# Experts' first products with the weights stationary in float16, and scatters cut to the rows set aside

## The chip, the cores and the metric

The kernel runs on one core of a Trainium2 chip. The metric is the device time of one execution in microseconds, as the median of the timed runs.

## The reference

One layer of a hybrid encoder over 2048 tokens of width 1024, with float32 inputs. The first sub-layer mixes tokens (latent attention, gated delta rule, pooling), projects, and ends in a layer norm. The second, on which this case turns, is a mixture of 32 experts in 4 groups:

```
h = x * (1.0 + sc2) + sh2
g_p, g_sel = lax.top_k(softmax(hf @ w_rg + b_rg), 1)          # one group of 4
e_p, e_idx = lax.top_k(softmax(logits of that group), 2)      # two experts of its 8
weights = g_p * e_p / jnp.sum(e_p, axis=-1, keepdims=True)
y[t] = sum over its two experts e of
       weights * ((silu(h[t] @ w_gate[e]) * (h[t] @ w_up[e])) @ w_down[e])
x = layer_norm(DEEPNORM_ALPHA * x + (1.0 + gt2) * y, ln2_g, ln2_b)
```

w_gate and w_up are 1024 x 256 per expert, w_down is 256 x 1024. There are 4096 assignments of a token to an expert.

## The kernel before

The program is one stream of instructions, written as Python generators; a planner orders each engine's instructions by expected durations and priority, and an engine then runs its queue in order. Only instructions marked `keep_in_program_order` stay where they are written.

The stages are: the input projection, the attention beside the delta rule, the output projection with the first norm and the routing (`phase_c`, some 1100 to 1345 us), the experts (`experts`, to 1848 us), and the final norm (`combine`). All matmuls on float32 data are done as three products of a high and a low part (`split`: ACT rounds the high part, DVE or POOL subtracts the low one), so that the sum is nearly exact.

Per tile of 128 tokens, `norm` (L1305) makes the experts' input h from the norm's rows g2 and b2, writes it to `s_h` in memory (L1325), and writes the residual, scaled, to `s_x1` (L1329). `route_tokens` and `routing` choose the experts, sort the experts by load into 32 places, and give each place a fixed number of blocks of 128 rows: three for places 0 and 1, two up to place 12, one beyond, 47 blocks in all. Rows without a token carry indices past the end: the gather skips them, and the scatter writes them to spare rows.

For each expert, `expert_load` (L1627) brings three pieces of 1 MB over SP's queue into one of two sets of three slots, and `expert_split` (L1636) cuts them into high and low parts (ACT and DVE, six pieces of 128 x 1024 each). A block is then:
- `gather` (L1647): POOL issues an indirect transfer of the block's rows of `s_h` into one of three buffers.
- `block_in` (L1662): eight float32 transposes on TensorE, and two splits of 128 x 512 out of PSUM into b_xH and b_xL.
- `block_gate` (L1673): 24 matmuls; the tokens are stationary and 512 columns of gate and up weights move. ACT takes the silu, DVE multiplies into b_hs.
- `block_mid` (L1686): two transposes of b_hs, and a split.
- `block_out` (L1696): 12 matmuls of 512 columns with w_down moving, scaled into b_yo by ACT and POOL (first half) and DVE (second half); then POOL issues an indirect transfer that adds b_yo's rows into `s_x1` (L1712).

TensorE's order in the steady loop (L1780) is: gate and up products of block n, transposes of block n + 1, down products of block n - 1. The work tiles (b_yo, b_hs and others) lie in two pools that alternate by block, with one buffer of b_yo in each. All scatters add into the same `s_x1`, so each one waits for the one before it. `overflow_tables` (L1808) prepares a loop (`overflow`, L1855) for experts that exceed their blocks; the loop's number of turns is read from data at the end.

## Time and profile before

| what | us |
|---|---|
| median of 3 runs (1896.87 to 1903.39) | 1901.23 |
| span of the profiled execution, first to last instruction | 1905.1 |
| TensorE busy in it | 1695.9 |
| VectorE busy in it | 1450.5 |
| ScalarE busy in it | 1019.4 |
| GpSimd busy in it | 792.0 |

The page of the profile gives a time for the profiled execution by its span alone. In the page PE is TensorE's matmuls and PEld its weight loads, DVE is VectorE, ACT ScalarE, POOL GpSimd, SP the engine that issues most transfers; L1712 is a line of the kernel. A row of a group has the number of instructions behind an x, then their busy time and the mean of one, then the idle time ahead of them. Matmuls overlap, so the mean of one is longer than the distance between two.

### The profile page before, as it was taken

The numbers are of one execution on the slowest core, as the hardware profiler recorded it, in microseconds if no ns is written. First come the engines' busy times: TensorE is split into PE (matmuls) and PEld (weight loads), VectorE is DVE, ScalarE is ACT, GpSimd is POOL, SyncE is SP. The second block draws the span as 40 slices with busy tenths as digits, with TensorE's granted clock in tenths as the row PEclk, the third lists the DMA queues.
The fourth block names the chain that finished last, engine by engine and source line by source line (L and its number), as shares of the span: only waits on it lengthen the run. The fifth ranks groups of instructions, "written<-read, shape, count | busy, mean of one in ns | idle before, by whom it ended". The sixth has DMA issues, their size and how long they took to land. (4 is left out here: it accounts for less than half of the span.)

```text
span 1905.1 us, 30525 instructions
## 1 busy us (share of the span) xinstructions
PE 1695.9 (89%) x10849; PEld 1341.0 (70%) x10849; DVE 1450.5 (76%) x2579; ACT 1019.4 (54%) x1785; POOL 792.0 (42%) x662
## 2 busy tenths in 40 slices
PE   6998999988999899999999798997689999999950
PEld 5776777666767687878777587776567788777740
DVE  7767667587878978777776387778579998988958
ACT  5522431256877787466667533233256666665737
POOL 0101126421667834344344353434424455544437
PEclk9999999999998999999999899998799999999985
DMA  9564123654432232332202643451398999999958
GB/s 350 177 200 152 67 75 119 195 171 166 119 83 65 54 71 65 95 81 79 69 26 75 206 166 134 144 189 68 126 323 249 313 306 307 310 292 306 324 123 339
DMA packets 173163, 322.71 MB, mean 169 GB/s; under 512 B 77617, under 2 KB 102737, under 8 KB 160716
## 3 DMA queue, kind: packets, MB, share of 16 engines
q1 hardware_dynamic: 151872, 261.33, 40.3%
q0 software_dynamic: 19008, 59.28, 12.3%
q8 instruction: 86, 1.41, 0.3%
q14 instruction: 69, 0.56, 0.1%
q10 hardware_dynamic: 2128, 0.13, 0.1%
HBM read 239.20 MB, written 89.01 MB: 172 GB/s over the span
## 5 line engine op out<-in xcount | busy, mean ns | idle before, releaser
L818 POOL TENSOR_TENSOR t_pL<-t_pt,t_pH 128x512 f16<-128x512 f32 (+3 forms) x153 | 158.1, 1037 | 232.6 <-ACT t_pH L816 144.7
L699 DVE TENSOR_REDUCE t_mp<-t_px 128x1 f32<-128x512 f32 (+2 forms) x320 | 190.6, 606 | 59.6 <-PE t_px L697 58.4
L815 ACT ACTIVATE t_pt<-t_stt 128x512 f32<-128x512 f32 (+1 forms) x320 | 172.1, 538 | 115.4 <-PE t_stt L811 101.4
L186 PE MATMUL a_mm<-hH,a_wH 128*128 128x512 f32 x448 | 182.6, 411 | 15.4 <-ACT hH L176 14.7
L120 DVE TENSOR_TENSOR e_w1L<-e_w,e_w1H 128x1024 fp32r<-128x1024 f32 x126 | 169.6, 1373 | 23.5 <-ACT e_w1H L119 23.4
L119 ACT ACTIVATE e_w1H<-e_w 128x1024 fp32r<-128x1024 f32 x128 | 133.1, 1063 | 85.0 <-PE b_pg L1680 65.3
L186 PE MATMUL a_mm<-hL,a_wH 128*128 128x512 f32 x448 | 171.8, 399 | 0.1
L816 ACT ACTIVATE t_pH<-t_stt 128x512 f16<-128x512 f32 (+1 forms) x320 | 171.5, 536 | 0.1
L186 PE MATMUL a_mm<-hH,a_wL 128*128 128x512 f32 x416 | 164.9, 399 | 2.2 <-DVE a_wL L120 2.2
L785 PEld LDWEIGHTS <-t_pH 128*128 128x128 f16 x2176 | 120.5, 99 | 59.6 <-issue 46.9
L1712 POOL DMA_INDIRECT s_x<-b_yo,q_idx x47 | 80.0, 1702 | 192.8 <-DMA s_x<-b_yo,q_idx 86.5
L1680 PE MATMUL b_pg<-e_w1H,b_xH 128*128 128x512 f32 x376 | 155.4, 413 | 0.5 <-ACT b_xH L119 0.5
L809 PE MATMUL t_stt<-qH,kH 96*128 96x512 f32 (+2 forms) x320 | 145.8, 456 | 7.2 <-ACT t_pH L816 7.2
L1680 PE MATMUL b_pg<-e_w1H,b_xL 128*128 128x512 f32 x376 | 151.5, 403 | 0.0
L1680 PE MATMUL b_pg<-e_w1L,b_xH 128*128 128x512 f32 x376 | 150.5, 400 | 0.0
L818 DVE TENSOR_TENSOR t_pL<-t_pt,t_pH 128x512 f16<-128x512 f32 (+3 forms) x167 | 121.0, 726 | 35.7 <-ACT t_pH L816 34.7
L785 PE MATMUL t_pv<-vH,t_pH 128*128 128x65 f16 x1088 | 138.1, 198 | 2.6 <-DVE t_yt L791 2.6
L785 PE MATMUL t_pv<-vH,t_pL 128*128 128x65 f16 x1088 | 134.8, 196 | 1.2 <-DVE t_pL L818 0.8
L697 PE MATMUL t_px<-kH,qH 96*128 96x512 f32 (+2 forms) x320 | 122.9, 393 | 13.0 <-DVE t_mp L699 11.0
L785 PE MATMUL t_pv<-vL,t_pH 128*128 128x65 f16 x1088 | 133.2, 194 | 0.0
L810 PE MATMUL t_stt<-qL,kH 96*128 96x512 f32 (+1 forms) x320 | 121.4, 379 | 0.0
L811 PE MATMUL t_stt<-qH,kL 97*128 97x512 f32 (+1 forms) x320 | 120.9, 378 | 0.0
(489 smaller groups left out, 4789.7 us busy)
## 6 DMA issues: line engine op xcount, KB each, us to landing
e_w<-moe_w SPq DMA_DIRECT2D x96, 1024.0 KB, 9.0
m_w<-w_modT SPq DMA_DIRECT2D x48, 512.0 KB, 4.4
c_xs<-x SPq DMA_DIRECT2D x16, 512.0 KB, 4.3
c_ys<-s_y SPq DMA_DIRECT2D x16, 512.0 KB, 5.0
s_h<-c_h SPq DMA_DIRECT2D x16, 512.0 KB, 2.6
s_x<-c_r SPq DMA_DIRECT2D x16, 512.0 KB, 2.6
f_x<-s_x SPq DMA_DIRECT2D x16, 512.0 KB, 10.1
out_dram<-f_x SPq DMA_DIRECT2D x16, 512.0 KB, 4.9
```

The source lines that it names most:

```text
L119: return (self.nc.scalar.activation(hi, src, AF.Copy), (eng or self.nc.vector).tensor_tensor(lo, src, f32(hi) if hi.dtype == F32R else hi, ...
L120: (eng or self.nc.vector).tensor_tensor(lo, src, f32(hi) if hi.dtype == F32R else hi, op=ALU.subtract))
L186: nc.tensor.matmul(pt, a[:, k, :], b[k][:, cc * CH:(cc + 1) * CH], start=k == 0 and n == 0, stop=k == KD - 1 and n == len(ops) - 1)
L697: pin(nc.tensor.matmul(px[:, 0:w], qH[0:r, t * P:(t + 1) * P], kH[e][0:r, kb * CH:kb * CH + w], start=True, stop=True))
L699: pin(v.reduce_max(mp[:, t, kb:kb + 1], px[:, 0:w], axis=AX.X))
L785: nc.tensor.matmul(pv[:, t, :], a[:, ts_], b[:, j, h, :], start=j == 0 and t == 0 and i == 0, stop=j == nj - 1 and t == 3 and i == 2, skip ...
L809: nc.tensor.matmul(st[:, off:], kH[e][0:r, js], qH[0:r, off:], start=True, stop=False)
L810: nc.tensor.matmul(st[:, off:], kH[e][0:96, js], qL[0:96, off:], start=False, stop=False)
L815: nc.scalar.activation(pt[:, off:], st[:, off:], AF.Exp, scale=SCALE)
L816: nc.scalar.activation(pH[:, off:], st[:, off:], AF.Exp, scale=SCALE)
L818: eng.tensor_tensor(pL[:, off:], pt[:, off:], pH[:, off:], op=ALU.subtract)
L1680: nc.tensor.matmul(pg, a[:, k], b[:, k], start=k == 0 and i == 0, stop=k == KD - 1 and i == 2)
```

## The change

Places get their own number of rows, in steps of 16 (`ROWS`, 4720 rows in all, still 47 blocks); an expert's one or two blocks become one unit of up to 256 rows, except that the three blocks of the first expert stay units of their own. For gate and up, the weights become stationary, in float16 high and low parts of the weights times 256, and the unit's tokens move, so the result comes out transposed already and `block_mid` goes. For that, `norm` scales h by a power of two and stores it as float16 high and low parts; `block_in` transposes those and copies them out of PSUM. Of the two pieces of w_down, the low part of one is now subtracted by POOL. The scatter moves only the rows set aside, and takes its indices through a column that tells whether the block's last element is finite; at the end, the loop for overflowing experts also redoes all blocks if a row was not. The work pools alternate by unit instead of by block. Weight pieces go through eight slots in turn instead of two sets of three; there are four gather buffers instead of three. The overflow tables have a tile of their own instead of borrowing b_yo.

The core of the diff:

```diff
-R3, R2 = 2, 13
-CAP = [3] * R3 + [2] * (R2 - R3) + [1] * (32 - R2)
+
+ROWS = [384] + [256] * 2 + [224, 208] + [192] * 2 + [176] * 5 + [160, 144] + [128] * 4 + [112] * 6 + [96] * 2 + \
+    [80] * 4 + [64] * 2
+CAP = [-(-n // 128) for n in ROWS]
+R3, R2 = CAP.index(2), CAP.index(1)
 NB = sum(CAP)
+
+NOV = 40
+
+WSC = 256.0
...
+            sig = self.sig = rp.tile([P, 4], F32, name="c_sig")
+            for i, src in enumerate((g2, b2)):
+                nc.scalar.activation(sc2, src, AF.Abs)
+                v.tensor_reduce(sig[:, i:i + 1], sc2, axis=AX.X, op=ALU.max)
+            v.tensor_scalar(sig[:, 0:1], sig[:, 0:1], sig[:, 1:2], 2.0 ** -60, op0=ALU.add, op1=ALU.max)
+            si = sig.bitcast(I32)
+            v.tensor_scalar(si[:, 0:1], si[:, 0:1], 0x7F800000, None, op0=ALU.bitwise_and)
+            v.tensor_scalar(si[:, 1:2], si[:, 0:1], float(13 << 23), None, op0=ALU.subtract)
+            v.tensor_scalar(si[:, 0:1], si[:, 0:1], -1.0, float(267 << 23), op0=ALU.mult, op1=ALU.add)
+            v.tensor_scalar(sig[:, 2:3], sig[:, 1:2], 1.0 / WSC, None, op0=ALU.mult)
+            nc.scalar.activation(g2, g2, AF.Copy, scale=sig[:, 0:1])
+            nc.scalar.activation(b2, b2, AF.Copy, scale=sig[:, 0:1])
+            self.identh = rp.tile([P, P], F16, name="c_identh")
+            v.tensor_copy(self.identh, c["ident"])
...
-                xs = X.pop(t)
-                r = wk.tile([P, D], F32, tag="r", name="c_r")
+                r = X.pop(t)
+                tmp = wk.tile([P, CH], F32, tag="r", name="c_r", bufs=1)
                 sums = wk.tile([P, 2], F32, tag="sum", name="c_sum")
                 for j in range(2):
                     js = slice(j * CH, (j + 1) * CH)
-                    v.tensor_tensor(r[:, js], pp.pop((t, j)), gt1[:, js], op=ALU.mult)
-                    v.scalar_tensor_tensor(r[:, js], xs[:, js], ALPHA, r[:, js], op0=ALU.mult, op1=ALU.add,
+                    v.tensor_tensor(tmp, pp.pop((t, j)), gt1[:, js], op=ALU.mult)
+                    v.scalar_tensor_tensor(r[:, js], r[:, js], ALPHA, tmp, op0=ALU.mult, op1=ALU.add,
                                            accum_out=sums[:, j:j + 1])
                 s = wk.tile([P, 5], F32, tag="ln", name="c_ln")
-                sq = wk.tile([P, D], BF, tag="lnq", name="c_lnq", bufs=1)
+                hx = wk.tile([P, 2, D], F16, tag="hx", name="c_hx", bufs=1)
...
-                nc.sync.dma_start(io["s_h"][sl, 0:D], h[t])
+                self.split(hx[:, 0], hx[:, 1], h[t], g_)
+                nc.sync.dma_start(io["s_h"][sl, 0:D], hx.rearrange("p a d -> p (a d)").bitcast(F32))
...
+        def first(k):
+            src, dst = w1[k // 4][:, k % 4:k % 4 + 2], slice(k, k + 2)
+            nc.scalar.activation(H[0][:, dst], src, AF.Copy, scale=WSC)
+            nc.vector.scalar_tensor_tensor(H[1][:, dst], src, WSC, H[0][:, dst], op0=ALU.mult, op1=ALU.subtract)
+        todo = [lambda k=k: first(k) for k in range(0, KD, 2)]
+        todo += [lambda k=k, e=e: self.split(H[2][:, k], H[3][:, k], w2[:, k], e)
+                 for k, e in enumerate((nc.gpsimd, nc.vector))]
...
+    def block_in(self, ps, x, off, xg):
+
         nc = self.nc
-        pg = ps.tile([P, CH], F32, tag="b_g", name="b_pg")
-        for k in range(KD):
-            if half and k == KD // 2:
+        m = xg.shape[0]
+        xh = xg[:, 0:D].bitcast(F16)
+        for i, copy in enumerate((lambda o, s: nc.scalar.activation(o, s, AF.Copy), nc.vector.tensor_copy)):
+            pt = ps.tile([P, KD, P], F16, tag="c_t", name="b_pt")
+            for k in range(KD):
+                nc.tensor.transpose(pt[:, k, 0:m], xh[:, i * D + k * P:i * D + (k + 1) * P], self.identh[0:m, 0:m])
+            copy(x[i][:, :, off:off + m], pt[:, :, 0:m])
+
+    def unit_gate(self, wk, ps, W, x, n, half=None):
...
+            pg = ps.tile([P, 2, 256], F32, tag="b_g", name="b_pg")
+            for j in range(2):
+                fs = slice((2 * j + f) * P, (2 * j + f + 1) * P)
+                for k in range(KD):
+                    for i, (a, b) in enumerate(((0, 0), (1, 0), (0, 1))):
+                        nc.tensor.matmul(pg[:, j, 0:n], W[a][:, k, fs], x[b][:, k, 0:n],
+                                         start=k == 0 and i == 0, stop=k == KD - 1 and i == 2)
+            hs = wk.tile([P, 256], F32, tag="hs", name="b_hs", bufs=2)
+            nc.scalar.activation(hs[:, 0:n], pg[:, 0, 0:n], AF.Silu, scale=inv)
+            nc.vector.scalar_tensor_tensor(hs[:, 0:n], pg[:, 1, 0:n], inv, hs[:, 0:n], op0=ALU.mult, op1=ALU.mult)
+            self.split(hH[:, f, 0:n], hL[:, f, 0:n], hs[:, 0:n])
...
+    def block_out(self, wk, ps, W, h, w, ms, col, first=False):
+
+        R, v = self.R, self.nc.vector
+        m = ms.stop - ms.start
+        yo = wk.tile([P, D], F32, tag="yo", name="b_yo")
+        self.block_rows(wk, ps, W, h, w, ms, yo, first)
+        ix = wk.tile([P, 1], I32, tag="ix", name="b_ix", bufs=2)
+        v.tensor_scalar(R["fin"][0:m, col:col + 1], yo[0:m, D - 1:D], 0.0, 0.0, op0=ALU.mult, op1=ALU.is_equal)
+        v.tensor_scalar(ix[0:m], R["dsp"][0:m, col:col + 1], R["fin"][0:m, col:col + 1], self.spare[0:m],
+                        op0=ALU.mult, op1=ALU.add)
+        self.scatter(yo[0:m], ix[0:m])
...
+        blocks, units = [], []
+        for i, r in enumerate(order):
+            bs = [(sum(CAP[:r]) + b, min(P, ROWS[r] - b * P)) for b in range(CAP[r])]
+            for u in ([b] for b in bs) if i == 0 else [bs]:
+                units.append((i, range(len(blocks), len(blocks) + len(u))))
+                blocks += u
+        slots = self.slots
+        loaded = [1]
...
+        def out(u, W, h, w, first=False):
+            off = 0
+            for n, wn in zip(units[u][1], w):
+                m = blocks[n][1]
+                self.block_out(wks[u % 2] if u > 1 else wks[0], ps, W, h, wn, slice(off, off + m), blocks[n][0], first)
+                off += m
...
+            h = self.unit_gate(wks[u % 2], ps, W[i], x, n)
+            if u == 4:
+                self.overflow_tables(rp, wks[u % 2])
             wn = w
-            if n + 1 < len(blocks):
-                x, w = block_in(n + 1)
-            if n + 3 < len(blocks):
-                self.gather(XG[n % 3], idx(n + 3))
-            for f in now[0::2]:
+            if u + 1 < len(units):
+                x, n, w = unit_in(u + 1)
+                gather(units[u + 1][1].stop + 4)
+            for f in todo[0::2]:
                 f()
             if prev:
-                self.block_out(wk(prev[0]), ps, *prev[1:])
-            h = self.block_mid(wk(n), pt, hs)
-            for f in now[1::2]:
+                out(*prev)
+            for f in todo[1::2]:
                 f()
-            prev = (n, W[i], h, wn, idx(n))
-        self.block_out(wk(prev[0]), ps, *prev[1:])
+            todo = []
+            prev = (u, W[i], h, wn)
+        out(*prev)
...
+        e32 = wk.tile([P, NOV, 32], F32, tag="ov", name="v_e32")
...
+            dsp = R["dsp"][:, 0:NB]
+            v.scalar_tensor_tensor(redo[:, 0:NB], R["fin"][:, 0:NB], 0.0, dsp, op0=ALU.is_equal, op1=ALU.mult)
+            v.memset(redo[:, NB:], 0.0)
+            v.tensor_scalar(redo, redo, self.spare, None, op0=ALU.add)
+            v.tensor_scalar(junk, redo, S + 0.5, 0.0, op0=ALU.is_lt, op1=ALU.add, accum_out=anyc[:, 0:1])
+            with ExitStack() as ep:
+                ps = ep.enter_context(self.pool(name="o_p0", bufs=1, space=PSUM))
+                pa = ps.tile([P, 1], F32, name="o_pa")
+                nc.tensor.matmul(pa, self.c["ones"], anyc[:, 0:1], start=True, stop=True)
+                v.tensor_scalar(anyc[:, 1:2], pa, 0.0, None, op0=ALU.is_gt)
+            flag = anyc[:, 1:2]
+            v.scalar_tensor_tensor(tab, R["tA"], flag, R["tB"], op0=ALU.mult, op1=ALU.add)
+            v.tensor_copy(tabi[:, 0:NB + NOV], tab[:, 1])
+            v.scalar_tensor_tensor(tabi[:, NB + NOV:], flag, float(NB), R["tot"], op0=ALU.mult, op1=ALU.add)
+            nov = nc.values_load(tabi[0:1, NB + NOV:NB + NOV + 1], min_val=0, max_val=NB + NOV)
```

## Rows read from the trace of the kernel before

**Rows 1.** Busy us by stage, PE to POOL; clock, DMA share, GB/s.

```profile
1100.00:1345.00 245.00, 219.29 (x1120) 181.62 (x1119) 193.48 (x412) 81.70 (x118) 111.03 (x87) 0.94 0.41 140
1415.00:1848.00 433.00, 408.98 (x1938) 329.23 (x1938) 384.02 (x494) 260.63 (x380) 202.95 (x126) 0.98 0.92 284
1500.00:1800.00 300.00, 290.76 (x1402) 234.49 (x1401) 273.40 (x337) 192.73 (x280) 147.61 (x92) 1.00 0.98 306
```

**Rows 2.** Chain that ended last, one block: start us, us, what.

```profile
1494.90 5.61 PE b_pg L1680 x24
1500.51 0.87 PE b_pt L1669 x8
1501.39 2.61 PE b_py L1704 x12
```

**Rows 3.** POOL's timeline: two neighbours, first and last of 38; [idle before].

```profile
1436.13 1.60 POOL L1712 DMA_INDIRECT s_x<-b_yo,q_idx  x1 [0.28 <-POOL b_yo L1709]
...
1497.38 1.59 POOL L1712 DMA_INDIRECT s_x<-b_yo,q_idx  x1 [6.37 <-DMA s_x<-b_yo,q_idx]
...
1504.27 1.59 POOL L1712 DMA_INDIRECT s_x<-b_yo,q_idx  x1 [1.96 <-DVE b_hs L1683]
...
1803.88 1.59 POOL L1712 DMA_INDIRECT s_x<-b_yo,q_idx  x1 [6.90 <-DVE b_wc L1658]
```

**Rows 4.** DMA view, 1497.4 and 1500:1800: count, us to landing.

```profile
s_x<-b_yo,q_idx POOLq DMA_INDIRECT x1, 6.1
...
s_x<-b_yo,q_idx POOLq DMA_INDIRECT x30, 9.0
```

**Rows 5.** Waits between 1415 and 1848: us in total, times, longest us.

```profile
ACT b_yo L1708 <- DMA s_x<-b_yo,q_idx: 39.1, 24, 2.7
...
DVE b_yo L1706 <- DMA s_x<-b_yo,q_idx: 15.5, 11, 1.9
```

**Rows 6.** Float16 in the attention: TensorE's timeline, and its loads as a group.

```profile
804.53 0.19 PE L785 MATMUL t_pv<-vH,t_pH 128*128 128x65 f16 x1
804.56 0.19 PE L785 MATMUL t_pv<-vH,t_pL 128*128 128x65 f16 x1
...
L785 PEld LDWEIGHTS <-t_pH 128*128 128x128 f16 x2176 | 120.5, 99 | 59.6 <-issue 46.9 <-DVE t_yt L791 5.0 <-DVE n_rt L1162 0.5
```

**Rows 7.** DMA view of the last scatter, 1847:1856.

```profile
q0 software_dynamic: 144, 0.52, 36.7%
...
s_x<-b_yo,q_idx POOLq DMA_INDIRECT x1, 6.2
```

**Rows 8.** First scatter's ACT and POOL timelines, 1358 to 1361 us.

```profile
1358.18 0.69 ACT L1708 ACTIVATE b_yo<-b_py,b_wc 128x512 f32<-128x512 f32 x1 [0.76 <-PE b_py L1704]
...
1360.51 1.69 POOL L1712 DMA_INDIRECT s_x<-b_yo,q_idx  x1 [0.30 <-POOL b_yo L1709]
```

**Rows 9.** Groups by line in 1100:1345, ACT and POOL.

```profile
L119 ACT ACTIVATE c_yH<-c_ys 128x1024 fp32r<-128x1024 f32 x14 | 14.8, 1055 | 69.7 <-PE c_pp L1280 54.5 <-DVE q_l L1579 12.3 <-DMA s_h<-c_h 2.8
...
L120 POOL TENSOR_TENSOR e_w1L<-e_w,e_w1H 128x1024 fp32r<-128x1024 f32 x2 | 4.9, 2448 | 0.0
```

**Rows 10.** DVE's timeline around the overflow tables.

```profile
1403.32 1.21 DVE L120 TENSOR_TENSOR e_w1L<-e_w,e_w1H 128x1024 fp32r<-128x1024 f32 x1
1412.04 0.69 DVE L1826 TENSOR_TENSOR v_e<-q_cnt,iotas 128x512 f32<-128x512 f32 x1 [7.52 <-DMA s_x<-b_yo,q_idx]
```

**Rows 11.** DVE's groups by line in 1500:1800.

```profile
L120 DVE TENSOR_TENSOR e_w2L<-e_w,e_w2H 128x1024 fp32r<-128x1024 f32 x42 | 54.6, 1300 | 2.0 <-ACT e_w2H L119 2.0
L120 DVE TENSOR_TENSOR b_xL<-b_pt,b_xH 128x512 fp32r<-128x512 f32 x60 | 38.2, 675 | 0.0
```

**Rows 12.** DVE's group in the final norm, 1855:1905.

```profile
L1929 DVE SCALAR_TENSOR_TENSOR f_x<-f_x,f_s,r_ln_g 128x1024 f32<-128x1024 f32 x16 | 19.9, 1277 | 17.1 <-DMA f_x<-s_x 17.0
```

**Rows 13.** POOL's and DVE's timelines at 1544.6.

```profile
1544.64 1.85 POOL L1709 TENSOR_TENSOR b_yo<-b_yo,r 128x512 f32<-128x512 f32 x1
...
1544.78 1.73 DVE L1658 SCALAR_TENSOR_TENSOR b_wc<-b_xg,q_eorf 128x2 f32<-128x2 f32 x1
```

More of the change, by code (lines that the diff above doesn't have):

```diff
@@ L1216, in phase_c @@
         R = self.R = {}
-        raw = self.raw = eo.enter_context(self.pool(name="raw", bufs=1, side="right"))
+        raw = eo.enter_context(self.pool(name="raw", bufs=1, side="right"))
+        self.slots = [(raw, "w%d" % i) for i in range(3)]
         pt = self.pt = eo.enter_context(self.pool(name="t_ps", bufs=2, space=PSUM))
@@ new lines, in expert_load @@
+        for i in range(3):
+            pool, tag = pieces(i)
+            t.append(pool.tile([P, 4, CH], F32, tag=tag, name="e_w%d" % (1 + i // 2)))
+            src = io["moe_w2"][bass.ds(ex, 1)] if i == 2 else io["moe_w1"][bass.ds(ex, 1), :, 4 * i:4 * i + 4]
+            dst = t[i] if i < 2 else t[i].rearrange("p a b -> p (a b)").rearrange("p (k f) -> p k f", k=2)
+            nc.sync.dma_start(dst, src.rearrange("e p k f -> (e p) k f"))
+        return t[:2], t[2].rearrange("p a b -> p (a b)").rearrange("p (k f) -> p k f", k=2)
@@ L1673, in block_gate @@
-    def block_gate(self, wk, ps, W, x, half=None):
-        nc = self.nc
-        pg = ps.tile([P, CH], F32, tag="b_g", name="b_pg")
-        for k in range(KD):
-            if half and k == KD // 2:
-                half()
-            for i, (a, b) in enumerate(((x[0], W[0]), (x[1], W[0]), (x[0], W[1]))):
-                nc.tensor.matmul(pg, a[:, k], b[:, k], start=k == 0 and i == 0, stop=k == KD - 1 and i == 2)
-        hs = wk.tile([P, 256], F32, tag="hs", name="b_hs")
-        nc.scalar.activation(hs, pg[:, 0:256], AF.Silu)
-        nc.vector.tensor_tensor(hs, pg[:, 256:CH], hs, op=ALU.mult)
-        return hs
@@ new lines, in unit_gate @@
+    def unit_gate(self, wk, ps, W, x, n, half=None):
+        nc = self.nc
+        hH = wk.tile([P, 2, 256], F32R, tag="hH", name="b_hH")
+        hL = wk.tile([P, 2, 256], F32R, tag="hL", name="b_hL")
+        inv = self.sig[:, 2:3]
+        for f in range(2):
+            if half and f:
+                half()
+            pg = ps.tile([P, 2, 256], F32, tag="b_g", name="b_pg")
[9 more added lines that the diff above has]
+            self.split(hH[:, f, 0:n], hL[:, f, 0:n], hs[:, 0:n])
@@ L1694, in block_mid, with block_rows @@
         return hH, hL
-    def block_out(self, wk, ps, W, h, w, idx, first=False):
+    def block_rows(self, wk, ps, W, h, w, ms, yo, first=False):
         nc = self.nc
-        yo = wk.tile([P, D], F32, tag="yo", name="b_yo")
+        m = ms.stop - ms.start
         for j in range(2):
@@ L1723, in experts @@
         xps = [pool("e_x0", "right")]
[L1724 removed]
+        gp = [pool("e_g%d" % i, "right") for i in range(4)]
         wks = [pool("e_k0", "right")]
@@ L1728, in experts @@
         order = [r for i in range(16) for r in (i, 16 + i)]
-        blocks = [(i, sum(CAP[:r]) + b) for i, r in enumerate(order) for b in range(CAP[r])]
-        raws, pt = [self.raw], self.pt
+        blocks, units = [], []
[4 more added lines that the diff above has]
+                blocks += u
@@ L1742, in block_in, with unit_in @@
-        def block_in(n):
-            r = order[blocks[n][0]]
-            ex = R["first"][:, 0:1] if n < 2 else R["eorf"][:, r:r + 1]
-            return self.block_in(xps[n % 2], pt, XG[n % 3]), self.block_weight(wk(n), XG[n % 3], ex)
+            return (R["idx1"] if n < 2 else R["idx"])[0:blocks[n][1], blocks[n][0]:blocks[n][0] + 1]
+        def unit_in(u):
+            r = order[units[u][0]]
+            ex = R["first"][:, 0:1] if u < 2 else R["eorf"][:, r:r + 1]
+            x = [xps[u % 2].tile([P, KD, 256], F16, tag="x" + t, name="b_x" + t) for t in "HL"]
+            w, off = [], 0
+            for n in units[u][1]:
+                m = blocks[n][1]
+                self.block_in(pt, x, off, rows(n))
+                w.append(self.block_weight(wks[u % 2] if u > 1 else wks[0], rows(n), ex[0:m]))
+                off += m
+            return x, off, w
@@ L1774, in experts, with gather @@
         wks.append(pool("e_k1"))
-        ws[1] = load(1)
-        for n in (3, 4):
-            self.tc.keep_in_program_order(self.gather(XG[n % 3], idx(n)))
+        ws = {1: load(1)}
+        nc.gpsimd.memset(XG[3], 0.0)
+        gathered = 3
+        def gather(upto):
+            nonlocal gathered
+            while gathered < min(upto, len(blocks)):
+                n = gathered
+                self.tc.keep_in_program_order(self.gather(rows(n), idx(n)))
+                gathered += 1
+        gather(5)
         todo = []
-        x, w = block_in(2)
-        for n, (i, b) in enumerate(blocks):
-            if n < 2:
+        prev = None
+        x, n, w = unit_in(2)
+        for u, (i, bs) in enumerate(units):
+            if u < 2:
                 continue
@@ L2106, in shape_consts @@
     z[:, 416] = S + 1 + i
+    z[:, 481] = S + i
+    for r in range(32):
+        lim = ROWS[r] if ROWS[r] % P else 1.0e6
+        z[:, 417 + r] = np.where(i // 32 == CAP[r] - 1, lim, 1.0e6)
+        z[:, 449 + r] = lim
     o["iotas"] = z
```

277 lines of the change are left out of this document (159 added, 118 removed).

## The prediction

> **What bounds the kernel now.** I read the stages first [rows 1]: the experts' blocks run from about 1415 to 1848 us, and in the steady 300 us of them TensorE is busy 97%, VectorE 91%, the 16 DMA engines 98%. Three candidates, so busy time alone names none. The chain of waits gives TensorE: a block is 5.6 us of gate and up products, 0.87 of transposes and 2.6 of down products [rows 2], 9.1 of the 9.9 us that a block takes. But that chain is followed backwards through semaphores, and it does not say who is full. So I looked at POOL's own timeline [rows 3] and at how long each scatter takes to land [rows 4]. The scatter issued at 1497.38 lands 6.1 us later, at 1503.48; the next is issued at 1504.27, 0.79 us behind it. Between 1436.13 and 1803.88 there are 38 scatters, so 37 intervals of 9.94 us on average; the landings have a median of 9.0 us [rows 4] and a mean of 9.1, and the rest is the gap, 0.75 to 0.84 us in nearly every case. The scatters are a serial chain without slack: each adds into s_x1 and waits for the one before. Their rows lie ready, and the back pressure reaches ACT and DVE, which wait for a scatter to land before they may overwrite b_yo (39.1 and 15.5 us) [rows 5]. TensorE is nearly as full, yet a cheaper matmul is worth no more than the scatter chain gives way.
>
> **The change part by part.** The page of the profile gives the profiled execution's span only (1905.1 us, 3.9 above the median of the timed runs); I sum against it and take the difference off the median.
>
> *Gate and up products.* Now 24 matmuls of 512 columns per block, 5.6 us [rows 2], some 2.2 columns per ns, 47 blocks: 261 us. After, a unit of n rows takes 96 matmuls of n columns, and the 32 places hold 4720 rows instead of 47 x 128 = 6016. Float16 in this form stands in the attention: 65 columns behind a weight load of their own start every 30 ns [rows 6], again 2.2 columns per ns. So 96 x 4720 / 2.2 = 206 us. Bounds: 96 x 34 units x 99 ns, if each product paid the whole busy time of its load, 310 us and above; 65/30 as it stands, 209. I take 206, as the rows are the same form.
>
> *The rest of TensorE.* Eight float32 transposes (0.87 us) become sixteen float16 ones of fewer columns, about 0.8 us by the same rate; the two transposes of b_hs go, with the waits ahead of them, the 0.8 us that the rows leave of a block; the down products stay at 12 of 512 columns. Together 206 + 47 x 3.6 = 375 us for 47 blocks, 8.0 per block against 9.9. TensorE no longer binds, so this saving is cover, not time.
>
> *Narrower scatters.* Behind the first expert's first two blocks, 45 scatters carry 4464 rows instead of 5760, 0.775 of them. The last scatter runs nearly alone: it lands in 6.2 us, of which its packets fill 36.7% of 9 us, 3.3 us; the other 2.9 is generation and latency [rows 7]. In the steady stretch 9.1 - 2.9 = 6.2 us therefore go with the rows, stretched by the weights' traffic: 6.2 x 0.225 = 1.4 us less per scatter. About 42 lie on the saturated chain: -59 us. Bounds: only the uncontended part shrinks, 3.3 x 0.225 x 42 = -31; everything shrinks, 9.1 x 0.225 x 42 = -86. I take the middle, since the landings of 6.1 and of 9.0 us [rows 4] show that the weights' traffic stretches the part that goes with the rows.
>
> *One b_yo for both blocks of a unit.* This is what the change adds. Today the two b_yo tiles alternate by block; after it they alternate by unit, so the second block of a two-block expert (places 1 to 13) may write b_yo only when its first block's scatter has landed. Now the gap from landing to next issue is 0.8 us; then ACT's write, POOL's product and the issue lie in it. Where nothing was in the way that took from 1358.18 to 1360.51, 2.3 us [rows 8], so at least 1.5 more. Behind other work it is an ACT split (1.05 us) [rows 9], a POOL subtraction of 128x1024 (2.45) [rows 9] and a DVE one (1.2) [rows 10] longer, 6.2 more in all. I take 3, as 2.4 us of POOL work is now queued there in only one place per expert: 13 x 3 = +39 us, bounds +20 and +81. Queued behind the waiting writes are, on ACT, the next weight splits and copies, and on DVE the same and the weights' release to SP's loads.
>
> *VectorE.* Per block 273.4 / 30.2 = 9.05 us now [rows 1]. Of every expert's two down-weight subtractions (1.30 us, [rows 11]) one moves to POOL: -0.9 per block. Two b_xL of 0.68 become one copy, by length 1.04: -0.3. The four up-weight pieces become fused operations; the nearest fused row of that length takes 1.28 [rows 12], an unhindered plain one 1.21 [rows 10]: +0.2. Two small operations for the validity column, 0.2 each: +0.4. Sum about 8.4 per block, hidden as long as the block lasts longer. What POOL's share does to it is weighed among the rivals.
>
> *DMA.* The scatters' own share shrinks by 3.3 x 0.225 = 0.74 us per block; the gathers fetch the tokens they fetched before; the weights are the same bytes in eight slots instead of six. 0.98 x 9.94 - 0.74 = 9.0 us per block: a floor below the new chain.
>
> *Around the stage.* The overflow tables no longer borrow b_yo: DVE's 7.5 us wait for a scatter before v_e goes [rows 10], while some 7 us of new table work come in; next in line there are the weights, so I take -5 (bounds -8, +3). In the norm stage each tile gains an ACT copy (1.05) and a POOL subtraction (2.4) [rows 9], and the tiles' scale some eight operations once. TensorE's 219 of 245 us cover the tiles [rows 1]; the last tile's 3.5 us, the scale's start, and the one buffer of the float16 halves, which the next tile's square has to wait for, are partly open: +4 (0 to +11). At the end, the new check of all blocks (a dozen small operations, 2 to 3 us) runs while the last scatter lands, 6.2 us [rows 7]; 0, or +3 if the loop's bound is read late. The inputs' loads per expert, counted by the reference's routing, are 276, 233, 224, 198, ... 46 in order, each within its place, so the overflow loop stays empty.
>
> Sum: -59 + 39 - 5 + 4 = -21, and -1 for the last scatter with its 64 rows: 1883 of 1905, or 1879 us by the median.
>
> **The rivals.**
> *The chain stops binding.* If the second block's wait costs only its minimum, the chain allows -59 + 20 = -39, and -86 + 20 = -66 with the whole landing shrinking; DMA's 9.0 us per block allow 42 x 0.94 = -39. With the surroundings (-2) -41, 1860 us. For it: the gap of 0.8 us is so regular that engines are not in the way today. Against: ACT and DVE are in order and full.
>
> *The wait blocks its engines: slower.* If ACT and DVE reach the second block's b_yo long before the scatter lands, both stand: a write ready some 2 us after the scatter's issue stands 5 us or more of a 7.7 us landing. 13 x 5 = 65 us of DVE idle, on 44 x 8.4 = 370 us of work and its usual idle of 9% (37 us): 472 against 433, +39 where all thirteen stand; at half of them +20, 1921 us, and that I take. It decides from 3 us of standing per two-block expert, the slack of VectorE over three blocks. For it: the same wait costs 1.6 us each time already (39.1 by 24) [rows 5], with one more block of distance. Against: the instruction order is planned from expected durations, and where the wait is expected other work is put ahead.
>
> *VectorE becomes the bound: no change.* At 1544.64 POOL starts a product of b_yo, at 1544.78 DVE a tiny operation on b_xg; it takes 1.73 us and ends with POOL's [rows 13]. The 32 subtractions given to POOL are of 2.45 us [rows 9]; if each blocks DVE for its length, 78 us or 1.8 per block: 8.4 + 1.8 = 10.2 against 9.94, 44 x 0.26 = +11; if three in four block, 9.8, -6. Between them 1901 us. Against: much of DVE's work reads PSUM, and those rows show no such stretch (0.68 us on average for b_xL) [rows 11]. In the Trainium skill, SBUF — State Buffer, section "Who interferes with whom", a DVE instruction with two SBUF inputs contends with a GpSimd instruction that reads SBUF, and the second to issue blocks; by that rule the four up-weight subtractions would all be open to it. The trace agrees for the row shown, 1.73 us.
>
> *Each product pays for its weight load.* At 99 ns for each of 3264 products 323 us and up instead of 206, TensorE at (323 + 169) / 47 = 10.5 us per block, 44 x 0.56 = +25 over today's pace, with the surroundings 1924 us. The rows against it are the 30 ns between float16 products [rows 6]. The Trainium skill (TensorE: Matmul & The Clock Gate, "Back-to-back issue gap") gives about 81 ns per matmul with its weight load at 128 columns; by it the 21 units of at most 128 rows would take some 65 us more than by 2.2 columns per ns (an estimate: 2016 products, 105 columns on average), and the trace disagrees, with 30 ns per pair at 65 columns [rows 6].
>
> **How the numbers follow.** Forecast 1879 with 0.48 (its own range 1862 to 1893); chain gone, 1860, 0.18; blocked engines, 1921, 0.20; VectorE, 1901, 0.08; weight loads, 1924, 0.06. The sum's extreme bounds are -86 + 20 - 8 = -74 and -31 + 81 + 3 + 14 = +67. Leaving out a tenth on each side gives 1845 to 1917. A measurement here tells about 0.3%, 5.7 us, from no change: faster takes the forecast but for a tenth of it and the first rival, 0.62; the same 0.13; slower 0.25.
>
> **What would show it.** Right: gate products that start every 50 to 110 ns; scatter landings about 7.7 us on average; gaps after a landing of 0.8 us twice, then some 4 us ahead of a second block's scatter; TensorE well under 90% busy between 1500 and 1800 us, with waits on others. Wrong: gaps that leave 0.8 us everywhere, or scatters that are issued long after the landing, which would mean the chain has slack; DVE idle of 5 us in front of b_yo; DVE's small operations stretched beyond 2 us in every block; landings as long as before in spite of fewer rows.

## The result: 2.35 times as long

The changed kernel takes 4453.9 us (median of 4 runs, 4449.9 to 4465.5) where the kernel before takes 1899.1 beside it: 2.347 times as long, 95% interval 2.340 to 2.354. The forecast was 1879 us.

The page of the changed kernel: its span, and of the 40 slices TensorE's busy tenths and the granted clock.

```profile
span 4454.1 us, 51620 instructions
...
PE   8999989998887777834443343334443344334441
...
PEclk9999999999898888865666555555655555655665
```

From the 18th slice on, at some 1900 us, the picture is another one: TensorE a third busy, its clock near the lower of its two levels (0.50 is 1.2 GHz), and that for 2500 us. The page's groups name what runs there; behind the bar are busy us and mean ns of one, then idle time and what ended it:

```profile
L126 DVE TENSOR_TENSOR o_w1L<-e_w,o_w1H 128x2048 fp32r<-128x2048 f32 x94 | 292.5, 3153 | 0.0
L2000 DVE COPY o_it<-o_tabi 128x1 int32 x47 | 7.2, 154 | 417.2 <-PEq L1987 410.1
L2019 DVE TENSOR_SCALAR o_l<-iotas,q_pos,o_mk 128x128 f16<-128x128 f32 x1504 | 455.9, 345 | 18.1
```

`o_it` is written once per turn of the overflow loop: 47 turns, one for each block set aside. DVE's timeline shows the first two turns begin 55.2 us apart, and how the flag that decides on them was worked out:

```profile
1913.19 2.45 DVE L1973 SCALAR_TENSOR_TENSOR o_redo<-q_fin,q_dsp 128x47 f32<-128x47 f32 x1
...
1915.95 0.20 DVE L1976 TENSOR_SCALAR_CACHE_REDUCE o_junk<-o_redo 128x48 f32<-128x48 f32 x1
...
1924.88 0.15 DVE L2000 COPY o_it<-o_tabi 128x1 int32 x1 [7.05 <-DMA s_x<-b_yo,b_ix]
...
1980.12 0.15 DVE L2000 COPY o_it<-o_tabi 128x1 int32 x1 [10.49 <-PEq L1987]
```

That is not all. The last scatter, 1847.19 before, comes at 1919.8. By stages, in the columns of [rows 1]:

```profile
1100.00:1345.00 245.00, 209.37 (x1035) 173.06 (x1036) 187.82 (x361) 85.71 (x119) 127.71 (x91) 0.91 0.38 129
...
1500.00:1800.00 300.00, 233.62 (x2462) 192.27 (x2460) 206.19 (x315) 157.07 (x230) 164.61 (x97) 0.86 0.81 252
1925.00:4420.00 2495.00, 988.35 (x3666) 636.00 (x3666) 1143.54 (x2452) 410.76 (x399) 507.65 (x244) 0.59 0.23 72
```

Between 1500 and 1800 every engine but POOL has less to show than in [rows 1], the DMA engines are busy 0.81 instead of 0.98, and the clock is no longer full. The waits of 1430:1850 (total us, times, longest) say where the engines stand; before, [rows 5] had 39.1 and 15.5 us for the first two, in about the same stretch (1415:1848):

```profile
ACT b_yo L1750 <- DMA s_x<-b_yo,b_ix: 91.8, 12, 11.1
DVE b_yo L1748 <- DMA s_x<-b_yo,b_ix: 75.2, 12, 10.7
POOL b_yo L1751 <- DVE b_yo L1748: 61.8, 10, 11.1
...
PEld b_py L1745 <- ACT b_yo L1750: 35.7, 8, 9.4
PE b_py L1745 <- ACT b_yo L1750: 34.5, 8, 9.3
```

So there are three places: a loop that should not run, some 45 us in the experts' stage, and some 28 in front of it (the first scatter is issued at 1389 to 1391 us, against 1360.51 in [rows 8]).

### The profile page after: what moved, and what is told of

Its sections match the earlier page's. It is cut to its first block, busy times and chain, and to the rows that moved or that the text cites. A ratio compares the mean times of both kernels' runs of the same rounds, so it can differ in the third digit from the quotient of the medians.

```text
span 4454.1 us, 51620 instructions
## 1 busy us (share of the span) xinstructions
PE 2656.5 (60%) x16935; PEld 1961.6 (44%) x16935; DVE 2584.0 (58%) x5119; ACT 1430.4 (32%) x2176; POOL 1396.9 (31%) x944
## 5 line engine op out<-in xcount | busy, mean ns | idle before, releaser
L2021 PE MATMUL o_pd<-tokh,o_l 128*128 128x1 f16 x1504 | 279.9, 186 | 695.6 <-DVE o_l L2019 639.9
L2019 DVE TENSOR_SCALAR o_l<-iotas,q_pos,o_mk 128x128 f16<-128x128 f32 x1504 | 455.9, 345 | 18.1
L126 POOL TENSOR_TENSOR o_w2L<-e_w,o_w2H 128x2048 fp32r<-128x2048 f32 x47 | 270.4, 5753 | 598.4 <-ACT o_w2H L125 598.4
L126 DVE TENSOR_TENSOR o_w1L<-e_w,o_w1H 128x2048 fp32r<-128x2048 f32 x94 | 292.5, 3153 | 0.0
L2044 PE MATMUL o_pg<-o_w1H,o_xH 128*128 128x512 f32 x376 | 188.6, 502 | 32.3 <-ACT o_xH L125 32.3
L1728 PE MATMUL b_pg<-b_xH,e_w1H 128*128 128x128 f16 (+11 forms) x1088 | 199.6, 228 | 6.1 <-ACT b_xH L1708 3.4
L1728 PE MATMUL b_pg<-b_xH,e_w1L 128*128 128x128 f16 (+11 forms) x1088 | 198.8, 227 | 0.3 <-DVE e_w1L L1682 0.3
L1728 PE MATMUL b_pg<-b_xL,e_w1H 128*128 128x128 f16 (+11 forms) x1088 | 196.9, 226 | 2.4 <-DVE b_xL L1712 2.4
L1682 DVE SCALAR_TENSOR_TENSOR e_w1L<-e_w,e_w1H 128x1024 f16<-128x1024 f32 x128 | 189.1, 1483 | 9.1 <-ACT e_w1H L1681 8.8
L192 PE MATMUL a_mm<-hH,a_wH 128*128 128x512 f32 x448 | 183.1, 412 | 15.6 <-ACT hH L182 14.8
L2044 PE MATMUL o_pg<-o_w1H,o_xL 128*128 128x512 f32 x376 | 185.1, 492 | 0.0
```

What stands on the lines that cost most here:

```text
L126: (eng or self.nc.vector).tensor_tensor(lo, src, f32(hi) if hi.dtype == F32R else hi, op=ALU.subtract))
L192: nc.tensor.matmul(pt, a[:, k, :], b[k][:, cc * CH:(cc + 1) * CH], start=k == 0 and n == 0, stop=k == KD - 1 and n == len(ops) - 1)
L1682: nc.vector.scalar_tensor_tensor(H[1][:, dst], src, WSC, H[0][:, dst], op0=ALU.mult, op1=ALU.subtract)
L1728: nc.tensor.matmul(pg[:, j, 0:n], W[a][:, k, fs], x[b][:, k, 0:n], start=k == 0 and i == 0, stop=k == KD - 1 and i == 2)
L2019: v.tensor_scalar(l, io128, R["pos"][:, k, t:t + 1], mk[:, k, t:t + 1], op0=ALU.is_equal, op1=ALU.mult)
L2021: nc.tensor.matmul(pd, l, self.tokh[:, t:t + 1], start=k == 0 and t == 0, stop=k == 1 and t == NT - 1)
```

## The experiments

"First" is the issue of the first scatter, "stage" the time from there to the last one, DMA share and clock are of 1500:1750 us, as the view prints them (a share can come out over 1). Ratios are to the kernel before, with 95% intervals. Executions of one kernel differ by 5 to 19 us between the lowest and the highest, so that a few us between two medians say nothing.

| run | us | ratio | first | stage | DMA | clock |
|---|---|---|---|---|---|---|
| before | 1899 to 1902 | 1 | 1360.5 | 486.7 | 0.97 | 1.00 |
| e1 loop's threshold | 1978.1 | 1.041 (1.037-1.045) | 1389.2 | 532.6 | 0.81 | 0.86 |
| e2 = e1, b_yo by block | 1976.5 | 1.041 (1.037-1.045) | 1389.4 | 526.8 | 0.81 | 0.86 |
| e3 = e1, no POOL piece | 2005.6 | 1.056 (1.052-1.060) | 1390.1 | 557.0 | 0.78 | 0.84 |
| e4 = e2 and e3 | 1938.0 | 1.020 (1.016-1.024) | 1391.4 | 488.5 | 0.87 | 0.90 |
| e5 = e4, square elsewhere | 1929.0 | 1.015 (1.012-1.019) | 1375.8 | 489.5 | 0.86 | 0.90 |
| e6 before, narrow scatters | 1883.0 | 0.991 (0.988-0.993) | 1360.0 | 465.4 | 0.95 | 1.00 |
| e7 before, b_yo by expert | 1982.6 | 1.043 (1.039-1.047) | 1358.4 | 562.3 | 0.80 | 0.93 |
| e8 = e5, two sums | 1936.2 | 1.019 (1.016-1.023) | 1396.1 | 453.7 | 0.93 | 0.92 |
| e9 = e5, four b_yo | 1929.7 | 1.015 (1.013-1.017) | 1379.0 | 494.4 | 0.90 | 0.91 |
| e10 = e5, blocks apart | 1916.4 | 1.010 (1.007-1.013) | 1373.5 | 478.7 | 0.90 | 0.92 |
| e11 = e9 and e10 | 1943.7 | 1.024 (1.022-1.026) | 1381.5 | 498.2 | 0.89 | 0.90 |
| e12 = e9, six b_ix | 1928.8 | 1.016 (1.012-1.019) | 1372.2 | 489.7 | 0.90 | 0.90 |
| e13 = e11, six b_ix | 1933.5 | 1.018 (1.015-1.022) | 1378.3 | 491.0 | 0.91 | 0.90 |
| e14 = e5, norm's low half on DVE | 1920.4 | 1.011 (1.007-1.015) | 1371.1 | 492.4 | 0.86 | 0.94 |
| e15 = e10, no check | 1916.2 | 1.008 (1.004-1.011) | 1379.2 | 488.0 | 0.89 | 0.92 |
| e16 = e12, 16 rows (leaves rows out) | 1859.4 | 0.978 (0.973-0.982) | 1375.9 | 426.1 | 0.86 | 0.97 |
| e17 = e10 and e14 | 1906.2 | 1.003 (1.001-1.006) | 1362.1 | 481.8 | 0.89 | 0.91 |
| e18 = e12 and e14, two sums | 1871.7 | 0.985 (0.983-0.988) | 1362.8 | 419.9 | 1.01 | 0.98 |

**The loop (e1).**

```diff
-            v.tensor_scalar(junk, redo, S + 0.5, 0.0, op0=ALU.is_lt, op1=ALU.add, accum_out=anyc[:, 0:1])
+            v.tensor_scalar(junk, redo, S - 0.5, 0.0, op0=ALU.is_lt, op1=ALU.add, accum_out=anyc[:, 0:1])
```

> One number is changed: the table that decides which blocks are done again counts as failed every entry below S - 0.5 = 2047.5 and no longer every entry below S + 0.5 = 2048.5. Theory (the threshold): an entry without a failure is the spare row, S + partition, which on partition 0 is 2048, under 2048.5; so the flag is always 1 and all 47 blocks are done again. With 2047.5 token rows alone (0 to 2047) count, the loop runs 0 turns (no o_it row at all), the some 2540 us of its 47 turns go, and what is left is the end of the last scatter, 1919.8 in the changed kernel, and the 54 us that stood behind it before: about 1970 us (1955 to 1985). Rival 1 (some rows really come out non-finite, or the comparison of 0 with the product misfires on the chip): the flag stays 1, 47 turns, 4450 us. Rival 2 (experts that exceed their rows): the loop runs as many turns as there are blocks too many, at 54 us each, between 1 and 40: 2020 to 4100 us.

1978.05 us, no turn of the loop, 2475.9 us less, as the theory had it. The flag was a slip of one in the code: an entry without a failure is `S + partition`, and on partition 0 that is below S + 0.5. Both rivals had kept turns.

**One b_yo per unit, POOL's subtraction (e2 to e4, e7).** e2 takes the tile of `block_out` from `wks[n % 2]` instead of `wks[u % 2]`; e3 is

```diff
-                 for k, e in enumerate((nc.gpsimd, nc.vector))]
+                 for k, e in enumerate((nc.vector, nc.vector))]
```

> As e1_no_loop, and the b_yo tile of a block is taken in turn by block instead of by unit: no more tiles, only the other order of the same two. Theory (the wait blocks its engines): the 92 us on ACT and 75 us on DVE of waits of b_yo for the scatter's landing shrink to under 40 and 20, the clock returns to 1.00, and the stage becomes shorter than before: 1850 to 1895 us. Rival (VectorE's subtractions beside POOL's, or the gate products, set the stage): the waits move elsewhere, less than 25 us come off e1: 1945 us and above.

> As e1_no_loop, and both halves of the down weights' low part are subtracted by VectorE, none by POOL. Theory (the wait of b_yo sets the stage): VectorE has about the same busy time (two at 1.2 to 1.3 us instead of one at 2.6), POOL issues each scatter sooner; within 15 us of e1, 1955 to 1975 us. Rival (the shared use of memory by VectorE and POOL sets it): 30 us and more off e1, under 1940.

> Both, b_yo by block and both subtractions on VectorE. Theory (the wait, and behind it scatters held up by POOL's 2.4 us piece): a little below e2, by 5 to 15 us: 1840 to 1885. Rival (VectorE becomes the bound without POOL's help): above e2, by as much as a subtraction per expert not hidden, 31 x 1.2 = 37 us at the most.

Neither alone brought anything (e2 within the interval of e1, e3 27.5 us slower, which no theory had), both together 40 us: the stage is then as long as before the change, 488.5 us against 486.7. The theories of e2 (1850 to 1895) and e4 (1840 to 1885) missed, by more than 50 us each. TensorE's waits of 1430:1850 show how the two hang together. In e1 it stands 46.3 us for a full b_py, which the writes of b_yo have to empty, and 26.4 us for a full b_pt, which VectorE's b_xL has to. e2 takes the first down to 16.4 and has this for the second; e3 takes the second down to 4.4 and has the next line for the first:

```profile
PE b_pt L1711 <- DVE b_xL L1712: 48.6, 9, 10.2
...
PE b_py L1745 <- ACT b_yo L1750: 99.4, 11, 11.1
```

In e4 they are 12.6 and 13.5 us. So each edit alone takes away one wait of TensorE while the other grows; why it grows is open. ACT's own wait of b_yo does not follow the time: it is 86.7 us in e1 and 110.3 in e4, which is 40 us faster. So b_yo by block is worth nothing beside POOL's piece (e1, e2), and 67.6 us without it (e3, e4). For the wait by itself the old kernel is the better place (e7):

```diff
-            self.block_out(wk(prev[0]), ps, *prev[1:])
+            self.block_out(wks[blocks[prev[0]][0] % 2], ps, *prev[1:])
```

> The kernel before with one change: the b_yo tile is taken in turn by expert instead of by block, as in the changed kernel. By the prediction's term 39 us more (20 to 81): 1940 us (1921 to 1982). Theory now (the wait stands in ACT's and DVE's queues, and TensorE stops behind the full b_py tiles): 50 to 80 us more, 1950 to 1980, with TensorE's clock below 1.00 in the stage. Rival (the new kernel's order alone makes the wait dear): under 20 us more.

82.9 us more (1982.6 against 1899.7), just above the range expected, and without any of the new products. Its waits of 1430:1850 carry the signature of the changed kernel, and on TensorE what stands behind them:

```profile
ACT b_yo L1708 <- DMA s_x<-b_yo,q_idx: 80.2, 11, 8.5
DVE b_yo L1706 <- DMA s_x<-b_yo,q_idx: 72.7, 11, 7.8
...
PEld b_pt L1669 <- DVE b_hL L120: 58.1, 11, 6.5
```

**Norm stage (e5, e14).** The waits of the changed kernel in 1100:1390 had a line that has no counterpart before, since there the square had a tile of its own:

```profile
ACT c_hx L1342 <- DMA s_h<-c_hx: 38.7, 7, 9.4
```

```diff
-                sq = hx[:, 1].bitcast(BF)
+                sq = tmp.bitcast(BF)
```

> As e4_yo_and_dve_split, and in the norm stage the squares are written into the scratch tile c_r instead of the second half of the float16 rows (c_hx), so that ScalarE's square no longer waits for the DMA that stores the rows of the tile before. Theory (that wait, 38.7 us in 7 times in e1, is most of the 26 us by which the norm stage is longer than in the kernel before): 15 us off e4, 1923 us (1915 to 1930), the last row tile stored some 10 to 20 us earlier. Rival (POOL's subtraction of 2.4 us per tile in the chain from the norm to the stored rows, or the residual's tile used in place): within 5 us of e4, 1933 to 1943.

9.0 us less by the medians: in the theory's range, though its 15 us were too many; in the profiled executions the first scatter comes 15.6 us earlier. e14 takes POOL's subtraction out of the chain of the norm:

```diff
-                self.split(hx[:, 0], hx[:, 1], h[t], g_)
+                self.split(hx[:, 0], hx[:, 1], h[t])
```

> As e5_square_elsewhere, and the norm stage's low halves (c_hx) are subtracted by VectorE (about 1.2 us per tile) instead of POOL (2.4). Theory (POOL's piece delays its three small operations of the next tile's norm, and TensorE's turn behind them): the norm stage gets 5 to 10 us shorter, 1921 us (1915 to 1925). Rival (VectorE is the fuller engine there, 18 of 20 us in every third stretch): longer by 5 to 15 us, 1935 to 1945.

8.6 us less by the medians, as the theory had it; in the profiled executions the first scatter comes 4.7 us earlier.

**Narrow scatters alone (e6).** The kernel before with `idx[0:rows]` and `yo[0:rows]` in the scatter, rows from the new ROWS.

> The kernel before with one change: its scatters carry the rows that the new kernel sets aside (16 to 128) instead of 128. By the prediction's term (1.4 us less per scatter on a saturated chain): 59 us less, 1842 us (1815 to 1870). Rival (what stretches a landing is the weights' traffic that it meets, not its own rows: in e4 landings of 112 rows take 9.7 to 13.1 us and some of 128 rows 6.3): 0 to 20 us less, 1880 to 1902.

16.7 us less (0.9905, interval 0.9877 to 0.9932): faster than both kernels, and a quarter of the forecast term. The landings of 1500:1800 went from a mean of 9.14 to 8.71 us, 0.43 and not 1.4 per scatter (they lie between 5.7 and 12.7 us, so that the 0.43 is rough); the median of the gaps stayed at 0.8. The DMA view of 1500:1800 has the median, 9.0 in [rows 4]; the row of the stage is in the columns of [rows 1]:

```profile
s_x<-b_yo,q_idx POOLq DMA_INDIRECT x32, 8.8
...
1500.00:1800.00 300.00, 297.88 (x1450) 244.37 (x1449) 264.23 (x355) 199.76 (x294) 149.00 (x94) 1.00 0.95 307
```

TensorE is at its limit there too, 297.88 of 300 us, so this run does not say what the chain alone would have given.

**Two sums (e8).** The blocks' scatters go in turn to s_x1 and s_x2; the last stage adds them. The Trainium skill, DMA: Bandwidth & Descriptors, "Rules for kernel authors", gives the reason to take a second tensor: a write that lands between an accumulating DMA's reading and writing of the same bytes is lost, so that a later one has to wait for the earlier. No run here tried that.

> As e5_square_elsewhere, and the blocks' scatters go in turn to two sums in memory, s_x1 and a second one, s_x2, that is filled with zeros during the attention and added in the last stage; so a scatter waits for the landing of the last but one. Theory (the serial chain of scatters still bounds the experts' stage, 9.9 us per block in e4): the stage falls to the next bound, the 16 DMA engines (0.86 of 9.9 = 8.5 us per block), 44 x 1.4 = 60 us less; the last stage reads 8 MB more, 15 to 25 us more: 35 to 45 us off e5, about 1883 (1865 to 1900). Rival (engines or DMA bound the stage and the chain only follows them): the stage stays, 15 to 25 us above e5, about 1940.

The stage fell by 36 us, 60 were expected, and the time rose by 7: the first scatter comes 20 us later, and from the last scatter to the end it takes 85 us instead of 56, with 8 MB more to read in the last stage. The 20 us I put down to the zeros, written from POOL's queue during the attention; in e18, which writes them from SP's, the first scatter comes at 1362.8.

**Who holds the scatters now (e9 to e13, e15).** e9: `bufs=2` for b_yo in both pools, five extra weight slots cut to four. e10 issues the down products of a unit's two blocks apart (the first ahead of the next unit's transposes, the second where both stood). e12: `bufs=6` for b_ix. e15 scatters by the static index.

> As e5_square_elsewhere, and four b_yo tiles instead of two (the memory for them comes from one of the eight weight slots). Theory (two b_yo, refilled in pairs by units of two blocks, make ACT stand 94 us for landings, with TensorE, DVE and the scatters' rows behind it): that wait falls under 20 us, scatters stand ready and the chain's gaps shrink from 2.3 to 0.8-1.0 us: 45 x 1.3 = 60 us at most, 25 to 45 off e5: 1890 us (1880 to 1905). Rival (the landings, 8.8 us in the mean, set the pace whatever stands ready, or a weight slot less delays the weights): within 10 us of e5, 1920 to 1940.

> As e5_square_elsewhere, and the down products of the two blocks of a unit are issued apart: the first right behind the next unit's gate products, the second after the next unit's rows are in, with half of the weights' splitting. Theory (pairs bunch the scatters, whose second waits out the first's landing): 10 to 25 us off e5: 1910 us (1900 to 1920). Rival (order of issue is not what holds them): within 8 us of e5.

> Both, four b_yo and the spread order. Theory: with four b_yo the order matters little, within 10 us of e9 (1880 to 1905). Rival: both gains add, 1870 to 1885.

e9 within 1 us of e5: its rival. e10 12.6 us less, as expected. Together (e11) they are slower than either, which neither theory nor rival had. In e9 the wait had found a new tile (`DVE b_ix <- DMA s_x`, 55.5 us in 17 times), so:

> As e9_four_yo, and six b_ix tiles (4 bytes a partition each) instead of two. Theory (in e9 VectorE stood 55 us in 17 writes of b_ix for a landing, and POOL 106 us behind it: a tile of 4 bytes took the place of b_yo as the bound): both waits go, and what four b_yo should have brought comes: 20 to 40 us off e9, about 1900 us (1890 to 1912). Rival (the landings beside the weights set the pace): the wait moves to POOL's s_x for s_x, within 10 us of e9 (1930).

> As e11_four_yo_spread, and six b_ix tiles. Theory: b_ix's wait was what made e11 slower than e10; 1943 falls to e10's 1916 or below, 1895 to 1918. Rival: the spread order with four b_yo is slow for another reason (PE's order of transposes that wait for the gathers, 53 us in e11): 1930 to 1945.

> As e10_blocks_spread, without the check of each block's rows (q_fin and b_ix left out: the scatters take the static index, and rows that are not finite would be added too). Theory (b_ix stands on VectorE behind weight pieces and holds the issue of the scatters, 16 us in 3 waits in e10): 8 to 20 us off e10: 1902 us (1896 to 1908). Rival (scatters wait for landings and for b_yo, not for b_ix): within 6 us of e10, 1910 to 1922.

All three came out with the rival: taking the column of finite rows out changes e10 by less than 1 us, and six b_ix change e9 by 1 us and e11 by 10, which still leaves it 17 us behind e10. But in e12 the chain is full, as before the change. POOL's timeline of three scatters, of 128, 64 and 112 rows by their place in the order:

```profile
1607.75 1.60 POOL L1756 DMA_INDIRECT s_x<-b_yo,b_ix  x1 [4.20 <-DVE b_hs L1732]
1621.03 1.45 POOL L1756 DMA_INDIRECT s_x<-b_yo,b_ix  x1 [11.68 <-DMA s_x<-b_yo,b_ix]
1626.68 1.53 POOL L1756 DMA_INDIRECT s_x<-b_yo,b_ix  x1 [0.49 <-DVE b_hL L126]
```

and the DMA view of the first two, issue to landing: queue, packets, MB, share of the 16 engines, then us to landing. The first, 1607.7:1620.3:

```profile
q1 hardware_dynamic: 423, 3.06, 68.0%
q0 software_dynamic: 208, 0.72, 28.0%
...
s_x<-b_yo,b_ix POOLq DMA_INDIRECT x1, 12.5
```

the second, 1621:1625.9:

```profile
q0 software_dynamic: 95, 0.32, 56.4%
...
q1 hardware_dynamic: 2, 0.01, 0.4%
...
s_x<-b_yo,b_ix POOLq DMA_INDIRECT x1, 4.9
```

The first shares the engines with 3 MB of weights (q1), the second has them alone. While the chain waits for the short one, no weights are under way. I read this as the splits that free the weights' slots standing in the same queues as the blocks. SP's own waits agree with that: between 1600 and 1640 three of them, 36.3 us in all and 17.2 at the longest, are ended by VectorE. It was not tried by itself.

**Sixteen rows (e16).**

```diff
-        self.scatter(yo[0:m], ix[0:m])
+        q = m if first else 16
+        self.scatter(yo[0:q], ix[0:q])
```

> As e12_four_yo_six_ix, but behind the first expert's two blocks each scatter carries only the first 16 of its rows (the other rows are left out of the sum). Theory (a landing is as long as the queue of weight traffic that it is issued into): landings beside streaming weights stay 7 to 11 us, and the time falls by 10 to 35 us, to 1895 to 1920 us. Rival (a landing goes with its own rows, as the prediction's 1.4 us for 29 rows has it): landings of 3 to 5 us, the chain drops out, and the stage falls to the weights' traffic, 3 MB per expert at some 390 GB/s or 5.4 us per block, and TensorE's 8.0: 60 us and more off, below 1870.

69.5 us off e12: the rival's side. With 16 rows the chain drops out (waits of s_x for a landing in 1430:1800: 13.7 us in 5 times, against 96.1 in 10 in e12). My theory that only the weights' traffic counts falls; a landing goes with its rows and with what it meets. In the three scatters above the long one has both, more rows and more weights. e14 has them the other way round, by the DMA view of 1622.8:1631.7 for 64 rows and of 1644.7:1651.9 for 128:

```profile
q1 hardware_dynamic: 405, 2.92, 79.2%
...
s_x<-b_yo,b_ix POOLq DMA_INDIRECT x1, 8.8
...
q1 hardware_dynamic: 50, 0.41, 13.6%
...
s_x<-b_yo,b_ix POOLq DMA_INDIRECT x1, 7.1
```

So 64 rows take 4.9 us without weights and 8.8 beside 2.9 MB, 128 rows 7.1 beside 0.4 MB and 12.5 beside 3.1.

**The last two (e17, e18).** e17 puts e10 and e14 together. e18 is e12 with e14's edit and two sums, zeroed in the norm stage from SP's queue.

> As e10_blocks_spread, with the norm stage's low halves on VectorE as in e14. Theory (separate stages): both gains, 13 and 8 us off e5: 1908 us (1902 to 1914). Rival (what the norm stage gains is lost in the wait for the first experts' weights): 1914 to 1920.

> As e12_four_yo_six_ix, with the norm stage's low halves on VectorE, and the scatters in turn to two sums as in e8, whose second is filled with zeros during the norm stage by SP's queue instead of POOL's. Theory (with rows standing ready the serial chain alone holds the stage at 10.2 us per block): the stage falls to 8.5 to 9.0 us per block, 44 x 1.4 = 60 us off, 8 off for the norm stage, 25 more in the last stage that reads 8 MB more: about 1885 us (1870 to 1902). Rival (the chain is full because the landings fill the DMA engines; two at a time land twice as late): 8 off, 25 more: 1935 to 1950.

e17, 1906.2 us: the gains of separate stages add up. e18, 1871.7 us, in the theory's range: 0.985 of the kernel before (0.983 to 0.988), the fastest that has all rows. Its 1500:1800, in the columns of [rows 1]:

```profile
1500.00:1800.00 300.00, 257.94 (x3184) 212.47 (x3181) 258.01 (x445) 203.19 (x304) 174.44 (x102) 0.96 0.97 320
```

A block takes 8.4 us between 1500 and 1750, against 10.2 in e12, and the DMA engines are full again, at 341 GB/s there instead of 303. Which engine is the bound now is not shown: between 1500 and 1750 ACT waits 6.7 us in all for weights, and TensorE is busy 229 of 250 us. The 8.4 us are less than the 9.1 that [rows 2] show for a block's old products, so I take it that the cheaper products are worth their change here; two sums in the kernel before, which would decide it, were not tried.

## Why the prediction was wrong, step by step

*The step that failed*: "the new check of all blocks ... 0, or +3" and "so the overflow loop stays empty". I counted the loads against the places, which holds (e1: no turn), and priced the operations of the check at 2 to 3 us beside a landing; they took 4.6 (1913.19 to 1917.8), were done before the last scatter was issued at 1919.8, and VectorE then stood 7.05 us until that had landed. I did not follow their arithmetic for a block without a failure. It stands in the diff: S + partition compared with S + 0.5; with S - 0.5 there the loop is empty and 2476 us go (e1). The loop was priced by whether it should run, not by what its bound would be: 2476 of the 2555 us, and no rival had it. The other 79 us lie outside the forecast's range too, and the terms below say why.

*One b_yo for both blocks of a unit*, +39, bounds +20 to +81: under-sized. By itself it costs 83 us in the kernel before (e7); in the changed kernel, 67.6 without POOL's piece (e3, e4) and nothing that can be measured beside it (e1, e2). The term priced the minimum path and one queued piece, 3 us; the writes stood 6.3 us (DVE) and 7.7 (ACT) on average, 12 times between 1430 and 1850. The rival "the wait blocks its engines" had the place and the mechanism, a standing of 5 us, and DVE's idle as its sign. It then halved the price because the order of issue is planned; 12 waits for 13 two-block experts do not bear that out.

*Narrower scatters*, -59: over-sized. Taking the fifth fewer rows off everything but the fixed 2.9 us assumed that a landing stretched by the weights shrinks in proportion. The weights' bytes stay, and the scatter still meets them (64 rows in 8.8 us beside 2.9 MB, e14): about -0.43 us per landing, -17 in all (e6, with TensorE full). My sign for it, landings "as long as before in spite of fewer rows", is nearly what e6 shows. *The chain stops binding*, the first rival, did not come: where rows stood ready (e12) the gaps were 0.75 to 0.9 us again.

*Gate and up products*: right in their price. In the changed kernel products of 224 columns start every 0.10 us and those of 64 columns every 0.03:

```profile
1500.93 0.27 PE L1728 MATMUL b_pg<-b_xL,e_w1H 128*128 128x224 f16 x1
1501.03 0.26 PE L1728 MATMUL b_pg<-b_xH,e_w1H 128*128 128x224 f16 x1
...
1901.03 0.19 PE L1728 MATMUL b_pg<-b_xL,e_w1H 128*128 128x64 f16 x1
1901.06 0.19 PE L1728 MATMUL b_pg<-b_xH,e_w1H 128*128 128x64 f16 x1
```

2.2 columns per ns, with a weight load for each; that rival is out. "Cover, not time" is not contradicted: e17, with the cheaper products and narrow scatters, is 23 us slower than e6 with the old products. But the products were not tried by themselves.

*VectorE*: less work than I had (206 us of 300 in the changed kernel, 7.8 per block where I had 8.4), not the bound; for the rest it waited. POOL's piece does lengthen DVE's:

```profile
L126 DVE TENSOR_TENSOR e_w2L<-e_w,e_w2H 128x1024 fp32r<-128x1024 f32 x18 | 46.1, 2558 | 11.9 <-ACT e_w2H L125 11.6
```

2558 ns where [rows 11] have 1300, and 1373 in e4, which has no such piece on POOL. The rule of the Trainium skill that the prediction named (SBUF — State Buffer, "Who interferes with whom") agrees with these numbers; what it is worth depends on the wait beside it (e3, e4).

*Around the stage*: the norm stage, +4 (0 to +11), cost 28 to the first scatter. The one buffer of the float16 halves was named and not priced: the next tile's square waits for their store, 38.7 us in 7 times. e5 and e14 bring the first scatter back to 1371, e17 to 1362.

*DMA*: the 9.0 us per block were no floor; e18 goes to 8.4, at 341 GB/s. The engines' share was 0.97 at 303 GB/s before, so a share near 1 does not fix what they move.

*Sums*: three figures of the prediction do not come out, and change nothing: 47 x 5.6 is 263, not 261; 96 x 34 x 99 ns is 323 us, not 310 (the rival has 323); 0.8 + 2.6 is 3.4 us, not 3.6. The -5 for the overflow tables no run tells apart.

What stays open: why with one of e2 and e3 alone the other wait grows, and why four b_yo and the spread order harm each other (e11, e13). All these change the planned order of five queues at once; steps of 10 us there I can't put to one cause.

## What to carry to other kernels

A loop that should be empty is part of the path: follow the value of its bound through one ordinary case, by hand, before pricing anything else. A buffer that is freed by a landing is priced with the whole landing, in every queue that writes it, and not with the path behind it. Before cutting the size of transfers in a serial chain, see what they share the engines with; a second destination that breaks the chain was worth more here than a fifth fewer rows, though only where rows stood ready (some 49 us, from e12 less e14's 8.6 to e18; alone, in e8, it lost 7).
